# Emptying TensorE's banks on ScalarE, a norm folded into a sigmoid's scale, and two smaller edits in the mixers of a decoder layer

## The chip, the cores and the metric

The kernel runs on one core of a Trainium2 chip. The core has five engines that run side by side, each with its own queue that is worked off in order: TensorE (PE) for matrix products, VectorE (DVE), ScalarE (ACT), GpSimd (POOL), and SyncE (SP), which issues most of the DMAs. Matrix products land in eight banks of PSUM, 128 partitions by 512 fp32 numbers each; everything else lives in SBUF, and inputs, outputs and scratch rows in DRAM. The metric is the device time of one execution in microseconds (us); lower is better.

## The reference, cut to what matters

One decoder layer on 512 rows of width 1024, all in float32: a norm, one wide projection, two mixers side by side, a gated sum, an output projection, and an MLP.

```
h = rms_norm(x, norm_mix_g);  p = h @ w_in
q_a, k_a, v_a, o_a, i_a, f_a, q_b, k_b, v_b, g_a, g_b = split(p)
qk_a = silu(causal_conv([q_a, k_a], conv_w))            # 4 taps
h_a = mlstm_chunkwise(q_a, k_a, v_a, i_a, f_a)          # 8 heads
y_a = sigmoid(o_a) * head_rms_norm(h_a)
qn, kn = head_rms_norm(q_b), head_rms_norm(k_b)         # per row and head of 128
z = qn . kn / sqrt(128);  beta = sigmoid(z)             # s < t only
y_b[t] = sum_s beta_ts * prod_{s<j<t} (1 - beta_tj) * v_s
y = sigmoid(g_a) * y_a + sigmoid(g_b) * y_b
x = x + y @ w_out;  h2 = rms_norm(x);  x = x + relu(h2 @ w_up)**2 @ w_down
```

## The kernel before

All large products run in a split form: each fp32 operand is written as a rounded high part plus the rest, and a product is three matmuls (`mm3`, lines 111 to 114). A weight tile is therefore loaded (`raw`), cast to its high part on ACT (line 107, `whi`) and subtracted to its low part on DVE (line 108, `wlo`). `stage` does this for a quarter of a projection chunk (256 input rows by 512 columns). Its `raw` tiles rotate through the buffers in `load_pool`, at first two of the pool `wp`; the high and low parts have four buffers each. With `pool_raw` a call puts its `raw` tile elsewhere; the opening does that for the first two quarters of `va0`, with the pool `xp`.

`chunk` multiplies one chunk: four banks of the pool `ps_proj` (all that it has) gather the products over four quarters, so the next chunk can start only as banks are emptied.

The work runs in four parts. The opening norms and transposes x into `hT`, multiplies `va0` and forms the gates' decay rows; its pools `xp` and `cv` are closed at line 317, and the room is used again by later pools. The mixers then run in the order of the list `ORDER` (line 52): `qka` and `qkb` are the chunks of queries and keys of the first and second mixer, `r` decay rows, `m` a head of the first mixer, `n` the norm over four of its heads, `T` transposes for two heads of the second mixer, `s` a head of it, and `va`, `vb`, `oa`, `ga`, `gb` the remaining chunks. Then come the output projection and the MLP. The list sets in which order steps are emitted; a planner places the instructions in each engine's queue from its own model of their times, and work marked with `high_priority(offset=AHEAD)` may be placed far ahead of its place in the list. Where an engine waits, everything behind in its queue waits too.

The steps that the change touches:

- `qka` (327): ACT empties the four banks into `xc` (333); DVE applies the four taps (339, 341), ACT takes sigmoids (343), DVE multiplies (345), and both split the results into `qh`, `ql`, `kk` (354 to 359) for the heads `m`. `xc` takes the four buffers with the tag "nat".
- `qkb` (445): DVE empties the four banks into `nat` (451), the same four buffers; ACT squares (453), DVE sums per row and head (454), ACT takes the root (456), DVE the reciprocal (457), and DVE scales queries and keys, 512 columns at a time (460). The 512 columns are two heads' queries and two heads' keys.
- `sb_transpose`, `pair_T`: PE turns `nat` head by head; ACT and DVE scale by the learned gain and split (468, 469).
- `sb_head`: z for one head lies in three banks, as four segments of 512, 384, 128 and 256 columns (`SEG`), one for each block of 128 queries, which stand on the partitions. ACT takes sigmoid(-z) and sigmoid(z) bank by bank (484, 485); POOL masks, DVE scans (493) and multiplies (494), PE transposes and multiplies by v.
- `mlstm_norm` (414): four heads' norms as an 8 by 512 tile `dd`, with the root on ACT (435) and the reciprocal on DVE (436); the result goes to DRAM (438) and is read back spread over 128 partitions, one row per head (441), and multiplied in on DVE (442). These DMAs are issued from SP's queue, as the weights' are.

Of the kernel before, what the change touches and what calls it, by code (L numbers as in the profile page):

```python
# [8 lines left out]
F32 = mybir.dt.float32  # L9
F32R = mybir.dt.float32r  # L10
AF = mybir.ActivationFunctionType
ALU = mybir.AluOpType
# [4 lines left out]
P = 128  # L17
# [39 lines left out]
def block_kernel(ctx: ExitStack, tc: tile.TileContext, x, norm_mix_g, w_in, b_if, b_gate, conv_w, mlstm_norm_g,  # L57
# [37 lines left out]
    def stage(k2, srcs, name, ahead=None, pool_raw=None):  # L95

        with tc.high_priority(offset=AHEAD if ahead is None else ahead):
            p, tag, bufs = load_pool[len(staged) % len(load_pool)] if pool_raw is None else (pool_raw, "raw", 2)
            staged.append(name)
            raw = p.tile([P, 2, 512], F32, tag=tag, name=f"raw_{name}{k2}", bufs=bufs)  # L100
            for c, ap in srcs:
                n = ap.shape[-1]
                last["load"] = nc.sync.dma_start(out=raw[:, :, c:c + n],
                                                 in_=ap.rearrange("(kk p) n -> p kk n", p=P)).ins
            hi = wp.tile([P, 2, 512], F32R, tag="whi", name=f"whi_{name}{k2}")
            lo = wp.tile([P, 2, 512], F32R, tag="wlo", name=f"wlo_{name}{k2}")
            act.copy(hi, raw)  # L107
            dve.tensor_sub(lo, raw, hi.bitcast(F32))  # L108
        return hi, lo
# [6 lines left out]
    def chunk(name, src, transposed, lhs=None, staged=None, evac=None, gen=False):  # L116


        acc = []

        def one(o, k, wh, wl):
            kk, sl = k % 2, slice(o * P, (o + 1) * P)
            st, sp = k == 0, k == NK - 1
            if transposed:
                mm3(acc[o], wh[:, kk, sl], wl[:, kk, sl], hT[0][:, k, :], hT[1][:, k, :], st, sp)
            else:
                ah, al = (hT[0][:, k, sl], hT[1][:, k, sl]) if lhs is None else lhs(k, sl)
                mm3(acc[o], ah, al, wh[:, kk, :], wl[:, kk, :], st, sp)

        def new(o):  # L130
            acc.append(ps_proj.tile([P, S], F32, tag="pp", name=f"pp_{name}{o}"))

        if evac is not None:
            w = staged or [stage(k2, src(k2), name) for k2 in range(4)]
            def each():
                for o in range(4):
                    new(o)
                    for k in range(NK):
                        one(o, k, *w[k // 2])
                    evac(o, acc[o])  # L140
                    yield
            if gen:
                return each()
            list(each())
        else:
            for o in range(4):
                new(o)
            for k2 in range(4):
                w = stage(k2, src(k2), name)
                for k in (2 * k2, 2 * k2 + 1):  # L150
                    for o in range(4):
                        one(o, k, *w)
        return acc
# [48 lines left out]
    def col(i):  # L202
        return vec[:, i:i + 1]
# [46 lines left out]
    def gates(wg):  # L250
# [37 lines left out]
        act.activation(em, em, AF.Exp)  # L288
        return cc, rows, em

    v0, v1 = [], []

    def v_evac(got, name):
# [20 lines left out]
    pe.transpose(pv[:, :NV], vec_r, ident[:NV, :NV])  # L314
    dve.tensor_copy(vec, pv[:, :NV])
    dve.tensor_scalar_mul(vec[:, 56:57], vec[:, 56:57], float(P) ** -0.5)
    first.close()

    oh = cst.tile([P, 8, 8], F32, name="oh")
# [6 lines left out]

    def qka(i):

        accs = chunk(f"qka{i}", in_cols((C_QA + 256 * i, 256), (C_KA + 256 * i, 256)), True)
        with tc.high_priority(offset=AHEAD):  # L330
            xc = [t2("nat", 4, f"xc{i}{o}") for o in range(4)]
            for o, a in enumerate(accs):
                taken = act.copy(xc[o], a).ins
        y = [t2("sy", 8, f"cy{i}{o}") for o in range(4)]
        for j in range(4):
            for o in range(4):
                w = col(24 + (0, 4)[o // 2] + 2 * i + o % 2 + 8 * (3 - j))
                if j == 0:
                    dve.tensor_scalar_mul(y[o], xc[o], w)
                else:  # L340
                    dve.scalar_tensor_tensor(y[o][:, j:], xc[o][:, :S - j], w, y[o][:, j:], ALU.mult, ALU.add)
        for o in range(4):
            last_sig = act.activation(xc[o], y[o], AF.Sigmoid).ins
        for o in range(4):
            dve.tensor_mul(y[o], y[o], xc[o])


        qh, ql, kk = [], [], []
        for o in range(2):
            q = r4.tile([P, 2, S], F32R, tag="r4", name=f"qh{i}{o}")  # L350
            k = r4.tile([P, 2, S], F32R, tag="r4", name=f"kk{i}{o}")
            l = r4.tile([P, 2, S], F32R, tag="r4", name=f"ql{i}{o}")
            for w, (a, b) in enumerate(((L, H), (H, L))):
                act.copy(q[a, w, :], y[o][a, :])
                dve.tensor_copy(q[b, w, :], y[o][a, :])
                pool.memset(l[b, w, :].bitcast(F32), 0.0)
                dve.tensor_sub(l[a, w, :], y[o][a, :], q[a, w, :].bitcast(F32))
                act.copy(k[a, w, :], y[2 + o][a, :])
                dve.tensor_sub(k[b, w, :], y[2 + o][a, :], k[a, w, :].bitcast(F32))
            qh.append(q)  # L360
            ql.append(l)
            kk.append(k)
        return qh, ql, kk, last_sig, taken
# [50 lines left out]
    def mlstm_norm(h0, ssum):  # L414
        pd = bank(f"pd{h0}")
        for i in range(4):
            t = r5(f"dh{h0 + i}")[:, :D].rearrange("p (w n) -> p w n", w=2)
            split(t, ssum[i])
            for w in range(2):
                pe.matmul(pd[:8, :], oh_r[:, h0 + i, :], t[:, w, :], start=(i + w == 0), stop=(i + w == 4))  # L420
        dd = at.tile([8, S], F32, tag="dd", name=f"dd{h0}", bufs=1)
        act.activation(dd, pd[:8, :], AF.Abs)
        dve.tensor_max(dd, dd, em)
        dve.scalar_tensor_tensor(dd, dd, EPS, dd, ALU.mult, ALU.mult)
        pq = bank(f"pq{h0}")
        for i in range(4):
            sq = t2("jk", 1, f"sq{h0 + i}")
            act.activation(sq, ya[h0 + i], AF.Square)
            t = r5(f"sh{h0 + i}")[:, :D].rearrange("p (w n) -> p w n", w=2)
            split(t, sq)  # L430
            for w in range(2):
                pe.matmul(pq[:8, :], oh_r[:, h0 + i, :], t[:, w, :], start=(i + w == 0), stop=(i + w == 4))
        dve.scalar_tensor_tensor(dd, pq[:8, :], 1.0 / P, dd, ALU.mult, ALU.add)
        dve.tensor_scalar_max(dd, dd, float(2.0 ** -116))
        act.activation(dd, dd, AF.Sqrt)
        dve.reciprocal(dd, dd)
        rr = dram.tile([8, S], F32, name=f"rr{h0}")
        nc.sync.dma_start(out=rr, in_=dd)
        for i in range(4):
            rt = t2("g", 2, f"rt{h0 + i}")  # L440
            nc.sync.dma_start(out=rt, in_=rr[h0 + i:h0 + i + 1, :].partition_broadcast(P))
            dve.scalar_tensor_tensor(ya[h0 + i], ya[h0 + i], col(h0 + i), rt, ALU.mult, ALU.mult)


    def qkb(p):
        acc = chunk(f"qkb{p}", in_cols((C_QB + 256 * p, 256), (C_KB + 256 * p, 256)), False)
        nat, r = [], sm.tile([P, 4, 4], F32, tag="ssq", name=f"ssq{p}")
        for t in range(NT):
            n = t2("nat", 4, f"nat{p}{t}")
            with tc.high_priority(offset=AHEAD):  # L450
                dve.tensor_copy(n, acc[t])  # L451
            jk = t2("jk", 1, f"njk{p}{t}")
            act.activation(jk, n, AF.Square)
            dve.tensor_reduce(r[:, t, :], jk[:, :].rearrange("p (s d) -> p s d", s=4), AX.X, ALU.add)
            nat.append(n)
        act.activation(r, r, AF.Sqrt, scale=1.0 / P, bias=eps)
        dve.reciprocal(r, r)
        for t in range(NT):
            n3 = nat[t][:, :].rearrange("p (s d) -> p s d", s=4)
            dve.tensor_tensor(n3, n3, r[:, t, :].unsqueeze(2).to_broadcast([P, 4, P]), ALU.mult)  # L460
        return nat

    def sb_transpose(nat, s, g, name):
        pt = bank(f"pt_{name}")
# [5 lines left out]
        return q  # L470

    def pair_T(nat, p):
        return [[sb_transpose(nat, 2 * w + i, 56 + w, f"{'qk'[w]}T{2 * p + i}") for w in range(2)] for i in range(2)]

    def sb_head(h, q, k, v):

        z = half_square(f"zb{h}_")
        for j, o, n in SEG:
# [1 line left out]
            mm3(part(z, o, n), q[:, 0, il], q[:, 1, il], k[:, 0, :n], k[:, 1, :n], j != 3, True,  # L480
                skip_group_check=True)
        b, r = f5(f"b{h}"), f5(f"r{h}")
        for zz, c, n in z:
            act.activation(r[:, c:c + n], zz[:, :n], AF.Sigmoid, scale=-1.0)  # L484
            act.activation(b[:, c:c + n], zz[:, :n], AF.Sigmoid)  # L485
        for j, o, n in SEG:
            d = slice(o + n - P, o + n)
            pool.affine_select(out=b[:, d], in_=b[:, d], pattern=[[-1, P]], compare_op=ALU.is_gt, fill=0.0, base=0,  # L488
# [388 lines left out]
```

## Time and profile before

| | |
|---|---|
| time, median of 3 runs | 835.6 us (834.01 to 836.1) |
| the profiled execution: time | 834.67 us |
| the profiled execution: span, first to last instruction | 833.0 us |
| mean granted TensorE clock | 0.996 |
| DMA traffic | 113.64 MB, mean 136 GB/s |

The span in 40 equal slices of 20.8 us, in tenths of full use:

```profile
PE   8999799999999999999999999999999999999998
DVE  5577878767586686857843649798689868978994
ACT  6337475754549456545633437567356635655541
PEclk9999899999999999999999999999999999999999
DMA  8165533334430523431256415867988896898963
```

The mixers fill slices 2 to 23, the MLP the rest. A busy digit is an average over a slice: an engine can be nine tenths busy and still have one short gap, and whether a gap matters depends on whether PE stands still in it. The granted clock is the share of its full clock that TensorE was given in a stretch. In the views, a row of waits reads "who, on which line, waited for whom: us in total, times, longest".

### The profile page before, as it was taken

To read this page: it belongs to the slowest core of one execution; us is meant where nothing else is said; L and a number is where in the kernel's file an instruction comes from. 1 tells how busy PE (TensorE), PEld (TensorE's weight loads), DVE (VectorE), ACT (ScalarE), POOL (GpSimd) and SP (SyncE) were. 2 spreads that over 40 slices of the span, in tenths; PEclk is the share of its full clock that TensorE was granted. 3 is DMA by queue.
4 is the path that set the end of the run, shared out by engine and by line. 5 is a ranking of instruction groups with operands and counts; after the bars stand their busy time and mean duration, and the time that the engine had idled before them with its cause. 6 is when DMAs were issued, how large, how long until landed. Compare 5 with 4: busy or idle time off the path is not lost.

```text
span 833.0 us, 11490 instructions
## 1 busy us (share of the span) xinstructions
PE 812.9 (98%) x4366; PEld 696.4 (84%) x4366; DVE 611.0 (73%) x815; ACT 450.4 (54%) x656; POOL 157.4 (19%) x214
## 2 busy tenths in 40 slices
PE   8999799999999999999999999999999999999998
PEld 5878588788887787878888889898999999999876
DVE  5577878767586686857843649798689868978994
ACT  6337475754549456545633437567356635655541
POOL 3013223102220330001120101222402330332220
PEclk9999899999999999999999999999999999999999
DMA  8165533334430523431256415867988896898963
GB/s 209 49 155 175 109 78 70 75 104 76 141 119 15 147 85 76 126 98 56 77 202 240 118 22 149 180 142 181 205 228 175 168 196 199 174 193 183 233 127 103
DMA packets 63849, 113.64 MB, mean 136 GB/s; under 512 B 5225, under 2 KB 17561, under 8 KB 63794
## 3 DMA queue, kind: packets, MB, share of 16 engines
q1 hardware_dynamic: 44210, 71.42, 30.3%
q0 software_dynamic: 19584, 41.50, 26.2%
q8 instruction: 34, 0.56, 0.3%
q14 instruction: 21, 0.17, 0.1%
HBM read 110.73 MB, written 2.17 MB: 136 GB/s over the span
## 4 chain that ended last, share of the span: by engine, by line
PE 78%; DVE 9%; ACT 5%; DMA 5%; issue 3%; SPq 0%; POOL 0%; ACTq 0%; DVEq 0%
PE pp_yup L112 3%; PE pp_yup L113 3%; PE pp_yup L114 3%; PE pp_qkb L112 3%; PE pp_qkb L114 3%; PE pp_qkb L113 2%; PE ydn L113 2%; PE ydn L112 2%; PE ydn L114 2%; DMA raw_qkb<-in_w_in_dram 2%; PE pp_gb L112 2%; PE pp_zup L113 2%; PE pp_zup L112 2%; PE pp_ga L112 2%; PE pp_ga L113 2%
## 5 line engine op out<-in xcount | busy, mean ns | idle before, releaser
L112 PE MATMUL pp_qkb<-whi_qkb,hT 128*128 128x512 f32 x128 | 50.6, 401 | 3.8 <-DVE nat L451 3.8
L488 POOL TENSOR_SCALAR_AFFINE_SELECT b<-b 128x128 f32<-128x128 f32 x32 | 18.8, 609 | 171.9 <-ACT b L485 156.2
L113 PE MATMUL pp_qkb<-wlo_qkb,hT 128*128 128x512 f32 x128 | 50.7, 396 | 0.0
L114 PE MATMUL pp_qkb<-whi_qkb,hT 128*128 128x512 f32 x128 | 50.4, 397 | 0.0
L679 POOL DMA_DIRECT2D raw_Xup<-in_w_up_dram x24 | 29.2, 1247 | 91.4 <-DVE wlo_p5up L644 43.0
L679 POOL DMA_DIRECT2D raw_Xdn<-in_w_down_dram x18 | 21.9, 1234 | 102.5 <-DVE wlo_p1dn L644 53.1
L493 DVE TENSOR_TENSOR_SCAN r<-r,msk 128x512 f32<-128x512 f32 (+3 forms) x32 | 25.0, 835 | 13.0 <-ACT r L484 12.8
L112 PEld LDWEIGHTS pp_qkb<-whi_qkb,hT 128*128 128x128 f32 x128 | 24.6, 192 | 9.0 <-DVE nat L451 4.0
L108 DVE TENSOR_TENSOR wlo_qkb<-raw_qkb,whi_qkb 128x1024 fp32r<-128x1024 f32 x16 | 19.4, 1222 | 16.7 <-ACT whi_qkb L107 16.7
L113 PEld LDWEIGHTS pp_qkb<-wlo_qkb,hT 128*128 128x128 f32 x128 | 24.5, 192 | 5.3
L114 PEld LDWEIGHTS pp_qkb<-whi_qkb,hT 128*128 128x128 f32 x128 | 24.5, 191 | 5.3
L802 ACT ACTIVATE uq<-uq 128x512 f32<-128x512 f32 x32 | 19.8, 630 | 14.2 <-DVE uq L801 14.1
L107 ACT CAST whi_qkb<-raw_qkb 128x1024 fp32r<-128x1024 f32 x16 | 16.6, 1048 | 18.5 <-DMA raw_qkb<-in_w_in_dram 11.5
L112 PE MATMUL pp_va<-whi_va,hT 128*128 128x512 f32 x64 | 25.6, 404 | 0.5 <-ACT g_ga L528 0.5
L112 PE MATMUL pp_gb<-hT,whi_gb 128*128 128x512 f32 x64 | 24.9, 391 | 1.1 <-DVE vb L170 1.1
L114 PE MATMUL pp_va<-whi_va,hT 128*128 128x512 f32 x64 | 25.5, 399 | 0.0
L113 PE MATMUL pp_va<-wlo_va,hT 128*128 128x512 f32 x64 | 25.5, 399 | 0.0
L114 PE MATMUL pp_oa<-hT,wlo_oa 128*128 128x512 f32 x64 | 25.2, 393 | 0.0
L113 PE MATMUL pp_qka<-hT,whi_qka 128*128 128x512 f32 x64 | 25.2, 393 | 0.0
L113 PE MATMUL pp_ga<-hT,whi_ga 128*128 128x512 f32 x64 | 25.2, 393 | 0.0
L113 PE MATMUL pp_oa<-hT,whi_oa 128*128 128x512 f32 x64 | 25.1, 392 | 0.0
L112 PE MATMUL pp_qka<-hT,whi_qka 128*128 128x512 f32 x64 | 25.1, 395 | 0.0
(570 smaller groups left out, 2969.2 us busy)
## 6 DMA issues: line engine op xcount, KB each, us to landing
raw_Xup<-in_w_up_dram POOLq DMA_DIRECT2D x24, 512.0 KB, 7.7
raw_Xdn<-in_w_down_dram POOLq DMA_DIRECT2D x18, 512.0 KB, 6.7
raw_qkb<-in_w_in_dram SPq DMA_DIRECT2D x32, 256.0 KB, 4.1
rb<-rows POOLq DMA_DIRECT2D x8, 640.0 KB, 5.1
raw_va<-in_w_in_dram SPq DMA_DIRECT2D x8, 512.0 KB, 3.8
raw_qka<-in_w_in_dram SPq DMA_DIRECT2D x16, 256.0 KB, 4.6
raw_vb<-in_w_in_dram SPq DMA_DIRECT2D x8, 512.0 KB, 4.7
raw_oa<-in_w_in_dram SPq DMA_DIRECT2D x8, 512.0 KB, 4.7
```

What stands on the lines that cost most here:

```text
L107: act.copy(hi, raw)
L108: dve.tensor_sub(lo, raw, hi.bitcast(F32))
L112: pe.matmul(o, ah, bh, start=start, stop=False, **kw)
L113: pe.matmul(o, ah, bl, start=False, stop=False, **kw)
L114: pe.matmul(o, al, bh, start=False, stop=stop, **kw)
L488: pool.affine_select(out=b[:, d], in_=b[:, d], pattern=[[-1, P]], compare_op=ALU.is_gt, fill=0.0, base=0, channel_multiplier=1)
L493: dve.tensor_tensor_scan(kr, kr, msk[:, S - n:][:, ::-1], 1.0, ALU.mult, ALU.max)
L679: pool.dma_start(out=buf[b, j], in_=src(more, j), accum_op=ALU.add)
L802: act.activation(h(r, c), h(r, c), AF.Square)
```

## The change

Four edits, all between the opening and the output projection.

1. The weights of `qka0` are staged before the opening's pools are closed, with the second and fourth `raw` tile in `xp`'s buffers; `chunk` takes the staged tiles.
2. The banks of `qkb` are emptied by ACT instead of DVE. (In `qka`, ACT does so already; there the loops over taps are written differently, and issue the same instructions.)
3. The queries are no longer scaled by their norm before the transposes. The norm's reciprocal, and its negative, are kept in a small tile `rq` and given to the sigmoids as the scale of each partition, so that the sigmoids run segment by segment, eight a head. The keys are scaled as before, one head at a time.
4. In `mlstm_norm` the four rows in use go to DRAM and come back as 16 columns on 128 partitions; root and reciprocal are taken there, and the result goes to DRAM and is spread as before.

```diff
@@ chunk
-                w = stage(k2, src(k2), name)
+                w = staged[k2] if staged else stage(k2, src(k2), name)
@@ end of the opening
+    def qka_src(i):
+        return in_cols((C_QA + 256 * i, 256), (C_KA + 256 * i, 256))
...
+    qka0_w = [stage(k2, qka_src(0)(k2), "qka0", None, xp if k2 % 2 else None) for k2 in range(4)]
     first.close()
@@ qka
-        accs = chunk(f"qka{i}", in_cols((C_QA + 256 * i, 256), (C_KA + 256 * i, 256)), True)
+        accs = chunk(f"qka{i}", qka_src(i), True, staged=qka0_w if i == 0 else None)
...
@@ mlstm_norm
-        act.activation(dd, dd, AF.Sqrt)
-        dve.reciprocal(dd, dd)
-        rr = dram.tile([8, S], F32, name=f"rr{h0}")
-        nc.sync.dma_start(out=rr, in_=dd)
+        rd_, rr = (dram.tile([4, S], F32, name=f"{n}{h0}") for n in ("rd", "rr"))
+        dq = at.tile([P, 16], F32, tag="dq", name=f"dq{h0}")
+        nc.sync.dma_start(out=rd_, in_=dd[h0:h0 + 4, :])
+        nc.sync.dma_start(out=dq, in_=rd_.rearrange("h (a b) -> (h a) b", b=16))
+        act.activation(dq, dq, AF.Sqrt)
+        dve.reciprocal(dq, dq)
+        nc.sync.dma_start(out=rr.rearrange("h (a b) -> (h a) b", b=16), in_=dq)
         for i in range(4):
             rt = t2("g", 2, f"rt{h0 + i}")
-            nc.sync.dma_start(out=rt, in_=rr[h0 + i:h0 + i + 1, :].partition_broadcast(P))
+            nc.sync.dma_start(out=rt, in_=rr[i:i + 1, :].partition_broadcast(P))
@@ qkb
             with tc.high_priority(offset=AHEAD):
-                dve.tensor_copy(n, acc[t])
+                act.copy(n, acc[t])
...
+        rq = at.tile([P, 2, 4, 2], F32, tag="rq", name=f"rq{p}", bufs=3)
+        dve.tensor_copy(rq[:, 0], r[:, :, 0:2])
+        dve.tensor_scalar_mul(rq[:, 1], r[:, :, 0:2], -1.0)
         for t in range(NT):
-            n3 = nat[t][:, :].rearrange("p (s d) -> p s d", s=4)
-            dve.tensor_tensor(n3, n3, r[:, t, :].unsqueeze(2).to_broadcast([P, 4, P]), ALU.mult)
-        return nat
+            for s in (2, 3):
+                n = nat[t][:, s * P:(s + 1) * P]
+                dve.tensor_scalar_mul(n, n, r[:, t, s:s + 1])
+        return nat, rq
@@ sb_head
-        for zz, c, n in z:
-            act.activation(r[:, c:c + n], zz[:, :n], AF.Sigmoid, scale=-1.0)
-            act.activation(b[:, c:c + n], zz[:, :n], AF.Sigmoid)
+        for j, o, n in SEG:
+            for w, d in ((1, r), (0, b)):
+                act.activation(d[:, o:o + n], part(z, o, n), AF.Sigmoid, scale=rq[:, w, 3 - j, h % 2:h % 2 + 1])
```

More of the change, by code (lines that the diff above doesn't have):

```diff
@@ L334, in qka, with tap @@
         y = [t2("sy", 8, f"cy{i}{o}") for o in range(4)]
-        for j in range(4):
-            for o in range(4):
[L337 to L341, printed above, removed]
+        def tap(o, j):
+            return col(24 + (0, 4)[o // 2] + 2 * i + o % 2 + 8 * (3 - j))
+        for o in range(4):
+            dve.tensor_scalar_mul(y[o], xc[o], tap(o, 0))
+        for j in range(1, 4):
+            for o in range(4):
+                dve.scalar_tensor_tensor(y[o][:, j:], xc[o][:, :S - j], tap(o, j), y[o][:, j:], ALU.mult, ALU.add)
         for o in range(4):
@@ L472, in pair_T, with sb_head @@
     def pair_T(nat, p):
-        return [[sb_transpose(nat, 2 * w + i, 56 + w, f"{'qk'[w]}T{2 * p + i}") for w in range(2)] for i in range(2)]
-    def sb_head(h, q, k, v):
+        nat, rq = nat
+        return [[sb_transpose(nat, 2 * w + i, 56 + w, f"{'qk'[w]}T{2 * p + i}") for w in range(2)] + [rq]
+                for i in range(2)]
+    def sb_head(h, q, k, rq, v):
         z = half_square(f"zb{h}_")
```

## The prediction

> **What bounds the kernel now.** First the busy shares on the page, then the stretches by time, then what TensorE (PE) waited for in the stretch of the mixers, then the instructions around its longest wait.
>
> ```profile
> span 833.0 us, 11490 instructions
> PE 812.9 (98%) x4366; PEld 696.4 (84%) x4366; DVE 611.0 (73%) x815; ACT 450.4 (54%) x656; POOL 157.4 (19%) x214
> ```
>
> PE is busy for 98% of the span, and the change touches no matmul. So it can win only what PE loses: idle time, and time at a lowered clock.
>
> The stretches (columns: window, its length, busy time and instruction count of each engine, granted TensorE clock, DMA share, GB/s):
>
> ```profile
> 38.00:84.00 46.00, 46.00 (x203) 37.16 (x202) 34.90 (x54) 25.94 (x39) 10.54 (x23) 1.00 0.56 151
> 87.40:94.40 7.00, 1.88 (x11) 1.26 (x9) 6.75 (x11) 2.32 (x4) 0.00 (x0) 0.81 0.53 94
> 94.40:98.40 4.00, 4.00 (x10) 3.13 (x11) 3.97 (x6) 1.22 (x2) 1.09 (x2) 0.50 0.46 97
> 38.00:480.00 442.00, 433.97 (x2067) 359.53 (x2066) 310.03 (x413) 239.61 (x368) 75.37 (x124) 0.99 0.41 111
> 190.00:240.00 50.00, 50.00 (x254) 42.59 (x253) 32.05 (x41) 21.20 (x37) 13.51 (x27) 1.00 0.41 115
> ```
>
> In the mixers (38 to 480) PE is idle for 442.00 - 433.97 = 8.0 us. Of this 7.00 - 1.88 = 5.1 us lie between 87.4 and 94.4. The next 4.0 us ran at clock 0.50, which loses another 4.0 x 0.5 = 2.0 us. So one place costs 7.1 us, and all the rest of the mixers 2.9 us. The waits of PE in the mixers (total, times, longest) say the same:
>
> ```profile
> PE pp_qkb L112 <- DVE nat L451: 3.8, 1, 3.8
> PE za L390 <- DVE kk L359: 1.3, 1, 1.3
> PE pp_gb L112 <- DVE vb L170: 1.1, 1, 1.1
> PE pn L112 <- ACT ph L399: 1.1, 1, 1.1
> PE pp_va L112 <- ACT g_ga L528: 0.5, 2, 0.3
> PE zb L112 <- DVE qT L469: 0.3, 1, 0.3
> ```
>
> The first two are that place: qkb1 can't start until VectorE (DVE) has emptied qkb0's banks (L451), and the head before it waits for kk. The timeline there (start, us, engine, line, operation, tiles, then idle before and its releaser):
>
> ```profile
> 87.48 0.69 DVE L345 TENSOR_TENSOR cy<-cy,xc 128x512 f32<-128x512 f32 x1
> ...
> 89.49 1.05 ACT L107 CAST whi_qkb<-raw_qkb 128x1024 fp32r<-128x1024 f32 x1
> ...
> 93.65 2.47 DVE L451 COPY nat<-pp_qkb 128x512 f32<-128x512 f32 x4
> 94.36 0.63 ACT L453 ACTIVATE njk<-nat 128x512 f32<-128x512 f32 x1 [3.83 <-DVE nat L451]
> ```
>
> Between L345 and L451 DVE works without a break (6.75 of 7.00 us in the window above) on qka0's results and on weights, while ScalarE (ACT) sits idle for 3.83 us. The copy is late because it stands in a long DVE queue, not because it is long.
>
> **Bank copies on ACT (L451).** Rows of the groups by line and shape (busy us, mean ns):
>
> ```profile
> L333 ACT COPY xc<-pp_qka 128x512 f32<-128x512 f32 x8 | 4.7, 585 | 3.1 <-PE pp_qka L114 2.7
> L451 DVE COPY nat<-pp_qkb 128x512 f32<-128x512 f32 x16 | 10.5, 685 | 2.4 <-PE pp_qkb L114 1.7 <-PE pt_kT L466 0.7
> L460 DVE TENSOR_TENSOR nat<-nat,ssq 128x512 f32<-128x512 f32 x16 | 12.2, 815 | 0.1
> ```
>
> The same copy of a bank costs ACT 585 ns, DVE 685. Moved, it adds 16 x 0.585 = 9.4 us to ACT and takes 11.0 us off DVE. In qkb0 two things hold the copy back. The four nat buffers are those of xc, whose last reader is L345, ended at 88.2. And ACT may first do its casts, which end at 89.49 + 1.05 = 90.5. With the copy first, PE restarts at 88.2 + 0.6 = 88.8 at the latest; with the casts first, near 91.1. Against 94.4 that is 5.6 or 3.3 us. Either wait is shorter than the present one, and the waits of 1.1 us elsewhere come with clock 1.00 in their stretches, so I count the 2.0 us of lowered clock as gone. The place gives 5.3 to 7.1 us (all of it, where the copies stand ready behind other PE work).
> The Trainium skill, "ScalarE: Activation LUTs", Rules for kernel authors, says to leave plain adds, multiplies and maxima to VectorE rather than ScalarE; by the same sense the copies belong on DVE, and of this place only the earlier loads' part, some 4 us, would be left. The two rows disagree for this fp32 copy out of a bank, 585 against 685 ns, and they decide.
>
> **First weights in the opening's buffers (L149).** Two of qka0's four raw buffers come from the opening's pool, so that its loads needn't wait for each other. Eight DMAs issue as before, in the same SP queue, only behind the opening's loads instead of later. A row of ACT's waits, and three of its timeline, show what this frees:
>
> ```profile
> ACT whi_qka L107 <- DMA raw_qka<-in_w_in_dram: 4.0, 2, 2.4
> 69.99 1.05 ACT L107 CAST whi_qkb<-raw_qkb 128x1024 fp32r<-128x1024 f32 x1 [4.06 <-DMA raw_qkb<-in_w_in_dram]
> 70.95 0.58 ACT L333 COPY xc<-pp_qka 128x512 f32<-128x512 f32 x1
> 71.42 5.55 ACT L381 ACTIVATE rb<-rb,cc 128x512 f32<-128x512 f32 x12
> ```
>
> Two casts of qka0 waited 4.0 us together for loads; PE lost nothing by it (46.00 of 46.00 from 38 to 84). What counts is the 4.06 us behind them: the last qkb0 load was late, and the fourth xc copy stands behind its cast on ACT. With qka0's raw buffers free some 5 us sooner (those 4.0 and a cast), qkb0's loads start sooner too, and up to 4.1 us of that wait goes. Then convolution, sigmoid and kk end up to 4 us earlier, which removes the za wait of 1.3 us and lets L345 free the nat buffers before PE is done with qkb0. So this edit works on the same place as the first, and together they can take no more than its 7.1 us. From between I take 6.3, nearer the top, since both work on it. If the load stays late, the copy edit's 5.3 remains. The two buffers hold the opening's room until qka0 is cast; the decay rows that come to lie over it are first used at 71.4, so nothing waits for it. The rewritten loops of the convolution issue the same instructions in the same order, and cost nothing.
>
> **The norm of the queries.** Per chunk, four multiplies of 128x512 (L460) become eight of 128x128 on the keys, and two small ones for the scales. Prices of single-source multiplies:
>
> ```profile
> L339 DVE TENSOR_SCALAR cy<-xc,vec 128x512 f32<-128x512 f32 x8 | 3.7, 499 | 1.4 <-ACT xc L333 1.4
> 56.55 0.15 DVE L316 TENSOR_SCALAR vec<-vec 128x1 f32<-128x1 f32 x1
> ```
>
> Between them, a 128x128 one is 0.15 to 0.50 us; I take 0.15 + 0.35/4 = 0.24, proportional to width. 32 x 0.24 = 7.7, and 8 x 0.2 = 1.6 for the scales, against 12.2 us: DVE saves 2.9 (from +5.4 to -5.8 by the bounds). Query transposes no longer wait for the norm. The sigmoids (L484, L485) go from six to eight a head, each with a scale from memory:
>
> ```profile
> 159.58 0.60 ACT L484 ACTIVATE r<-zb 128x512 f32<-128x512 f32 x1
> ...
> 162.22 1.28 ACT L435 ACT_TABLE_LOAD   x1
> ```
>
> Six take 162.22 - 159.58 = 2.64 us now. The twelve exponentials of L381 above, in the same four widths and with an operand per partition, took 5.55 us, so four are 1.85 and eight 3.7. That is +1.06 a head, 8.5 us on ACT in all, and 1 us more before each head's transposes. What hides it is the projection matmuls that run between: from 190 to 240, with heads in it, PE lost nothing. Uncovered it would be up to 8.5 us.
>
> **The reciprocal over 128 partitions (n0, n4).** The rows, and the SP queue around both:
>
> ```profile
> L436 DVE RECIPROCAL dd<-dd 8x512 f32<-8x512 f32 x2 | 6.7, 3342 | 1.3 <-ACT dd L435 1.3
> L457 DVE RECIPROCAL ssq<-ssq 128x16 f32<-128x16 f32 x4 | 1.0, 247 | 0.4 <-ACT ssq L456 0.4
> 170.05 0.30 SPq L438 DMA_DIRECT2D rr<-dd  x1
> ...
> 172.12 1.06 SPq L441 DMA_DIRECT2D rt<-rr  x2
> ...
> 342.91 0.30 SPq L438 DMA_DIRECT2D rr<-dd  x1
> 344.37 0.83 SPq L441 DMA_DIRECT2D rt<-rr  x2
> wg_r<-in_w_in_dram SPq DMA_DIRECT2D x1, 64.0 KB, 13.0
> ```
>
> The DVE operation falls from 3.34 to 0.25 us, 6.2 in all. Two DMA hops are added (out, and back spread over 128 partitions). One hop, issue to the issue that waits for it, is 2.07 us at n0 and 1.46 at n4. So a chain gains 3.1 and loses 2.9 to 4.1: about even, up to +1.0. New waits: SP stands two hops longer before the next weight loads, ACT waits for a DMA at the root (casts of transposed weights behind it), DVE at the reciprocal (behind it the casts' remainders, and later qT, for which PE already waits 0.3 us). The far end for a hop in 64-byte pieces is wg_r's 13.0 us, which is eight times the bytes (64 KB against 8) behind the opening's megabytes in the same queue; the hop of dd itself, 16 KB between the same stages, is nearer, so I keep 1.5 to 2.1 and no loss.
> The Trainium skill, "DMA: Bandwidth & Descriptors", Specifications, has pieces under 512 B pay a read-modify-write; 64-byte pieces fall under it. No row of this kernel prices that at an idle queue; as a mechanism it is the rival of the longer round trip below.
>
> **Sum.** DVE in the mixers: -11.0 - 2.9 - 6.2 = -20 of 310 us; ACT +9.4 + 8.5 = +18 of 240. Both stay far under 442, so neither becomes the bound on average. PE: -6.3 at 87 to 98, the four other waits (3.0) unchanged in sum, and +0.5 for new small waits, since a planner lays out all queues anew: -5.8. Against the profiled execution, 833.0 span and 834.67 with what lies around it, this gives 828.9. That execution is 0.9 below the median of the runs, 835.6, so I forecast **829.8**, with 827 to 832 as its own range.
>
> **Rivals.**
> *All small waits go too* (DVE is 20 us lighter; the vb wait stands behind DVE's work): 7.1 + 3.0 = 10.1, so 825.5. Against it: they have four different causes, two of them on ACT. Chance 0.12.
> *Half of it*: the copies stand behind ACT's casts and kk, and the za wait stays; 3.3 us, or less with a new wait elsewhere: 832.3. For it: 88.2 as L345's end stays if the late load stays. Chance 0.18.
> *No gain, the change does not do what it says*: the planner puts copies behind exponentials or sigmoids (5.55 us in one go on ACT at 71.4), and PE waits as long, only for ACT: 835.6. Chance 0.13.
> *Slower*: the round trip of n0 and n4. If ACT stands at the root for both hops with the copies of transposed weights and qkb3's banks behind it, PE runs out: two waits of 4.1 us, each long enough for the lowered clock (2.0 more, as at 94.4), 12.2 - 5.8 = +6.4, so 842. It decides once a hop exceeds what PE has queued; at equal price the break-even is 2.9 us lost at each. By the page named above hops get longer and this is what would show. Against it: n0's chain today has 3.34 us in one piece and PE waits only 0.3 there. Chance 0.13.
> The forecast itself has 0.44.
>
> Differences under about 0.3%, 2.5 us, can't be told from no change here. Faster means below 833.1: 0.44 + 0.12 + two thirds of the half case, and a little of the rest: 0.69. Slower means above 838.1: 0.13 and a little of the third: 0.14. Same: 0.17. The range runs from 823.5 (every wait gone, with 2 us more for rows too coarse) to 837 (no gain), leaving out the slower case.
>
> **What would show it.** Right: clock 1.00 throughout 80 to 105, pp_qkb waiting under 1 us for ACT nat, the wait for raw_qkb before xc under 1 us, the reciprocal at 0.25 us and no PE wait over 1 us near n0 and n4. Wrong: a PE wait of 3 us or more anywhere in the mixers, a clock below 1 behind it, or zb waiting for sigmoids.

## Result and profile after

| | before | changed |
|---|---|---|
| time, median (range) | 834.89 us (834.01 to 836.1, 4 runs) | 825.49 us (824.51 to 825.58, 4 runs) |
| ratio to before, 95% interval | | 0.9892 [0.9878, 0.9906] |
| the profiled execution: time / span | 834.67 / 833.0 us | 825.4 / 823.3 us |

The changed kernel is 9.4 us faster. That lies inside the range, outside the forecast's own band of 827 to 832, and on the rival "all small waits go too" (825.5). The head of the page of the changed kernel, and its row of the granted clock in 40 slices:

```profile
span 823.3 us, 11511 instructions
...
PE 809.8 (98%) x4366; PEld 694.6 (84%) x4366; DVE 595.3 (72%) x823; ACT 458.0 (56%) x683; POOL 164.6 (20%) x214
...
PEclk9999999999999999999999999999999999999999
```

The one 8 in the clock row, the slice of qkb1, has gone. PE does the same 4366 matmuls. The stretches of the changed kernel (columns as in the prediction):

```profile
87.40:94.40 7.00, 7.00 (x35) 5.92 (x34) 6.91 (x10) 3.64 (x7) 2.94 (x4) 1.00 0.41 75
94.40:98.40 4.00, 4.00 (x25) 3.56 (x23) 3.30 (x5) 2.28 (x3) 1.38 (x2) 1.00 0.81 144
38.00:470.00 432.00, 430.57 (x2064) 357.71 (x2063) 294.34 (x421) 247.24 (x395) 82.61 (x124) 1.00 0.42 111
470.00:823.00 353.00, 345.33 (x2169) 311.03 (x2168) 282.19 (x370) 192.78 (x259) 75.27 (x62) 1.00 0.77 168
```

What was the hole at 87 to 98 is full (7.00 of 7.00, 4.00 of 4.00) at clock 1.00. Over the mixers, now 432 us long, PE is idle for 432.00 - 430.57 = 1.43 us, where it was 8.03. That is 6.6 us of idle time, and with the 2.0 us of lowered clock 8.6 of the 9.7 us by which the two spans differ. The output projection and the MLP, 353 us, kept their PE work within 0.3 us (345.09 of the same 353.00 before):

```profile
480.00:833.00 353.00, 345.09 (x2169) 311.16 (x2167) 282.26 (x370) 192.85 (x259) 75.27 (x62) 1.00 0.77 168
```

All that PE waited for in the mixers of the changed kernel, the whole answer of the view:

```profile
PE po L113 <- DVE al L521: 1.4, 1, 1.4
```

So the two waits at qkb1 are gone as forecast, but so are the four others (vb 1.1, ph 1.1, g_ga 0.5, qT 0.3), which the forecast had left standing. One wait is new. A second profile of the changed kernel (the run changed_again below) has this wait at 1.9 and two more of 0.3 and 0.2, so a difference of half a microsecond between the waits of two profiles says little. Two rows of ACT's timeline at qkb0's banks in the changed kernel show the copies (DVE's stood at 93.65):

```profile
85.32 0.59 ACT L461 COPY nat<-pp_qkb 128x512 f32<-128x512 f32 x1
86.48 1.54 ACT L461 COPY nat<-pp_qkb 128x512 f32<-128x512 f32 x3
```

The last copy ends at 86.48 + 1.54 = 88.0, 5.6 us before the old group began, and before PE starts qkb1 at 88.37.

### The profile page after: what moved, and what is told of

The parts are those of the page before. It is cut to its first block, busy times and chain, and to the rows that moved or that the text cites. A ratio compares the mean times of both kernels' runs of the same rounds, so it can differ in the third digit from the quotient of the medians.

```text
span 823.3 us, 11511 instructions
## 1 busy us (share of the span) xinstructions
PE 809.8 (98%) x4366; PEld 694.6 (84%) x4366; DVE 595.3 (72%) x823; ACT 458.0 (56%) x683; POOL 164.6 (20%) x214
## 4 chain that ended last, share of the span: by engine, by line
PE 91%; DVE 4%; DMA 3%; issue 1%; ACT 1%; SPq 0%; ACTq 0%; DVEq 0%
PE pp_qkb L114 4%; PE pp_qkb L112 4%; PE pp_qkb L113 4%; PE pp_yup L112 3%; PE pp_yup L113 3%; PE pp_yup L114 3%; PE ydn L112 2%; PE ydn L114 2%; PE ydn L113 2%; PE pp_qka L112 2%; PE pp_va L112 2%; PE pp_qka L113 2%; PE pp_va L113 2%; PE pp_va L114 2%; PE pp_zup L113 2%; PE pp_zup L112 2%
## 5 line engine op out<-in xcount | busy, mean ns | idle before, releaser
L114 PE MATMUL pp_qkb<-whi_qkb,hT 128*128 128x512 f32 x128 | 50.0, 393 | 0.0
L112 PE MATMUL pp_qkb<-whi_qkb,hT 128*128 128x512 f32 x128 | 49.3, 392 | 0.0
L108 DVE TENSOR_TENSOR wlo_qkb<-raw_qkb,whi_qkb 128x1024 fp32r<-128x1024 f32 x16 | 21.7, 1364 | 13.4 <-ACT whi_qkb L107 13.3
L112 PE MATMUL pp_ga<-hT,whi_ga 128*128 128x512 f32 x64 | 25.3, 395 | 0.0
L113 PE MATMUL pp_wo<-wlo_wo,y 128*128 128x512 f32 x64 | 25.1, 392 | 0.0
L113 PE MATMUL pp_ga<-hT,whi_ga 128*128 128x512 f32 x64 | 25.1, 392 | 0.0
```

The lines of the kernel that those rows point to most:

```text
L112: pe.matmul(o, ah, bh, start=start, stop=False, **kw)
L113: pe.matmul(o, ah, bl, start=False, stop=False, **kw)
L114: pe.matmul(o, al, bh, start=False, stop=stop, **kw)
```

## Experiments

Three questions. Are the gains of the four edits independent? Why did the vb, ph, g_ga and qT waits go? What is the new wait worth? The theory in front: edits 1 and 2 win the place at qkb1, and the small waits went because each of them hangs on a queue that two or more of the edits shorten. Its rivals: DVE is simply lighter, so that edit 3 or 4 alone would remove some of these waits; and the changed order of the planner's queues did it, with no single cause. The eight kernels with a single edit or without one keep the convolution's loops as they were, which issue the same instructions.

**Four single edits**, each put alone into the kernel before. Their cores:

```diff
only_staging:
+    qka0_w = [stage(k2, qka_src(0)(k2), "qka0", None, xp if k2 % 2 else None) for k2 in range(4)]
only_act_copies:
-                dve.tensor_copy(n, acc[t])
+                act.copy(n, acc[t])
only_sigmoid_scale:
+            act.activation(d[:, o:o + n], part(z, o, n), AF.Sigmoid, scale=rq[:, w, 3 - j, h % 2:h % 2 + 1])
only_reciprocal:
+        act.activation(dq, dq, AF.Sqrt)
+        dve.reciprocal(dq, dq)
```

> The kernel before with the first edit alone (qka0's weights staged in the opening's buffers). One-place theory (the gain is the single stop at qkb1's start, and edits 1 and 2 both work on it): the fourth xc copy comes about 4 us earlier, DVE ends its queue about 4 us earlier and still copies the banks, so PE restarts near 90.3 instead of 94.4 and the clock stays at 1.00: -4 to -6 us against before. Rival (the gain is DVE's lighter load, 20 us in the mixers): this edit takes no work off DVE, so at most -1 us.

> The kernel before with the second edit alone (qkb's banks emptied by ACT). One-place theory: PE restarts at 88.8 (copy ahead of ACT's casts) to 91.1 (behind them), the lowered clock goes: -5 to -7 us against before, and the late load of qkb0 stays visible as ACT's 4 us wait before the fourth xc copy. Rival (lighter DVE): 11 of the 20 us go, so about half of the 9.4 us, spread over several waits and not at one place.

> The kernel before with the third edit alone (queries' norm as the sigmoid's scale). One-place theory: nothing of the stop at qkb1's start goes, 0 +- 1 us against before. Rival (lighter DVE): -1 to -2 us. If the sigmoids' extra microsecond a head is not covered: up to +8 us.

> The kernel before with the fourth edit alone (root and reciprocal over 128 partitions). One-place theory: 0 +- 1 us against before; if the changed kernel's PE wait of 1.4 us for DVE al in n0 comes from the round trip, it shows here too and this edit alone is +1 to +2 us. Rival (lighter DVE): the vb wait of 1.1 us goes, -1 us.

**The changed kernel without one edit** (the same hunks taken back, one at a time):

```diff
without_staging:
-    qka0_w = [stage(k2, qka_src(0)(k2), "qka0", None, xp if k2 % 2 else None) for k2 in range(4)]
without_act_copies:
-                act.copy(n, acc[t])
+                dve.tensor_copy(n, acc[t])
without_sigmoid_scale:
+            dve.tensor_tensor(n3, n3, r[:, t, :].unsqueeze(2).to_broadcast([P, 4, P]), ALU.mult)
without_reciprocal:
+        act.activation(dd, dd, AF.Sqrt)
+        dve.reciprocal(dd, dd)
```

> The changed kernel without the first edit. One-place theory: as the copies alone, some -5 to -7 us against before (828 to 830), with ACT's 4 us wait for the last qkb0 load back. If the two edits only replace one another at that place, it is within 1 us of the changed kernel, 825 to 826.5.

> The changed kernel without the second edit: DVE empties qkb's banks. One-place theory: as the staging alone, -4 to -6 us against before (829 to 831). Lighter-DVE theory: 9 of the 20 us remain, about -4 us, but not at the stop of qkb1.

> The changed kernel without the third edit. One-place theory: within 1 us of the changed kernel, 824.5 to 826.5. If this edit is what removed the small waits near 255 and 274 us, those are back and it is 827 to 828.

> The changed kernel without the fourth edit. If the round trip causes the PE wait of 1.4 us for DVE al in n0, that wait goes and it is 823.5 to 824.5; if the edit is what removed the vb wait of 1.1 us near 355, that is back and the two cancel, 825 to 826.

Measured, with the waits of PE in the mixers (us, from the view of waits of one profiled execution of each kernel; the medians are over all its runs; "qkb1" is the wait of pp_qkb for nat, "za" for kk, "ph" that of pn for ph; waits of 0.2 are left out):

| kernel | median us | ratio [95%] | qkb1 | za | vb | ph | others |
|---|---|---|---|---|---|---|---|
| before (profile) | 834.9 | 1 | 3.8 | 1.3 | 1.1 | 1.1 | g_ga 0.5, qT 0.3 |
| only_staging | 829.85 | 0.9938 [0.9923, 0.9953] | 2.4 | - | 1.5 | 0.8 | g_ga 0.5, qT 0.4 |
| only_act_copies | 832.71 | 0.997 [0.9954, 0.9985] | - | 0.7 | 2.7 | 1.0 | g_ga 0.5 |
| only_sigmoid_scale | 841.5 | 1.0079 [1.0062, 1.0096] | 3.8 | 1.0 | 0.6 | 5.0 | qT 0.3 |
| only_reciprocal | 837.95 | 1.0036 [1.0023, 1.0049] | 3.8 | 0.6 | 2.8 | 1.0 | g_ga 0.5, qT 0.4 |
| without_staging | 828.0 | 0.9933 [0.9916, 0.995] | - | 1.3 | - | - | al 1.0, pl 0.5, nat 0.5 |
| without_act_copies | 829.21 | 0.9951 [0.9936, 0.9966] | 1.7 | - | 1.9 | - | qT 0.5 |
| without_sigmoid_scale | 825.27 | 0.9908 [0.9889, 0.9926] | - | - | 0.5 | 1.3 | g_ga 0.5, pl 0.5 |
| without_reciprocal | 829.25 | 0.996 [0.9945, 0.9975] | - | - | 2.5 | - | kT 2.1 |
| changed | 825.49 | 0.9892 [0.9878, 0.9906] | - | - | - | - | al 1.4 |

The medians of before beside them were 834.82 for the single edits and 833.23 for the four that leave one out. Against them, the single edits give -5.0, -2.1, +6.7 and +3.1: in sum +2.7, while together they give -9.4. Edits 3 and 4, each a loss alone, cost nothing or gain in company: by the ratios (each kernel to the before measured beside it) the changed kernel without edit 4 is slower by 0.68% (5.7 us), without edit 3 by 0.16%, within the intervals. Without edit 2 it loses 0.59% (4.9 us), without edit 1 0.41% (3.4).

*The place at qkb1.* DVE's timeline in only_staging:

```profile
89.62 2.47 DVE L455 COPY nat<-pp_qkb 128x512 f32<-128x512 f32 x4
```

The same group stood at 93.65: 4.03 us earlier, just the late load's 4.06. PE's wait shrank from 3.8 to 2.4 and the clock stayed up. PE's stretch there, then two of only_act_copies (window, length, PE busy, clock, DMA share, GB/s):

```profile
84.00:106.00 22.00, 19.64 (x95) 1.00 0.43 99
```

```profile
84.00:106.00 22.00, 21.07 (x99) 1.00 0.52 113
350.00:400.00 50.00, 47.33 (x235) 0.97 0.26 75
```

Alone, staging leaves 22.00 - 19.64 = 2.4 of the place's 7.1 us, and the whole kernel gains 5.0. The copies alone leave 22.00 - 21.07 = 0.9, so they win 6.2 there, but the kernel gains only 2.1. Its second row shows where the rest went: between 350 and 400 PE lost 2.67 us idle and 50 x 0.03 = 1.5 to the clock, where the kernel before lost 1.08 and none:

```profile
350.00:400.00 50.00, 48.92 (x248) 1.00 0.31 89
```

That is the wait for vb, grown from 1.1 to 2.7. So the first half of the theory holds, and the vb wait is where gains are given back.

*The vb wait.* It is 0.5 or none where edits 2 and 4 stand together (without_staging, without_sigmoid_scale, changed), and 0.6 to 2.8 elsewhere in the table; the 0.6, of edit 3 alone, can't be told from the 0.5. DVE at the end of n4 in only_reciprocal shows what holds vb:

```profile
355.36 0.75 DVE L446 SCALAR_TENSOR_TENSOR yq<-yq,vec,rt 128x512 f32<-128x512 f32 x1 [1.49 <-DMA rt<-rr]
356.03 1.88 DVE L170 TENSOR_TENSOR vb<-pp_vb,vb 128x512 fp32r<-128x512 f32 x3
```

vb's remainders stand in DVE's queue behind n4's multiplies, and these wait for a DMA of the norm. So n4's chain can set PE's wait. Since the kernels reach n4 at different times, the chain is measured from PE's last matmul of its squares (pq) to the issue of rr. In the changed kernel, PE, SP's queue and ACT:

```profile
324.15 0.40 PE L438 MATMUL pq<-sh,oh_r 128*8 128x512 f32 x1
```

```profile
325.75 0.27 SPq L444 DMA_DIRECT2D rd<-dd  x1
329.25 0.35 SPq L445 DMA_DIRECT2D dq<-rd  x1
332.79 0.33 SPq L448 DMA_DIRECT2D rr<-dq  x1
334.24 0.80 SPq L451 DMA_DIRECT2D rt<-rr  x2
```

```profile
330.97 1.28 ACT L446 ACT_TABLE_LOAD   x1
332.26 0.22 ACT L446 ACTIVATE dq<-dq 128x16 f32<-128x16 f32 x1
```

dd leaves 325.75 - 324.15 = 1.6 us behind the last square. The root has to wait for ACT in any case, which runs a head's sigmoids and squares and loads a table until 332.25; dq, 1.7 us on its way from 329.25, is there by then, and the root has no wait for a DMA in its row. Both hops lie beneath ACT's work, and rr goes out 332.79 - 324.15 = 8.6 us behind the last square. In only_reciprocal, PE and SP's queue:

```profile
330.59 0.39 PE L432 MATMUL pq<-sh,oh_r 128*8 128x512 f32 x1
```

```profile
337.12 0.27 SPq L438 DMA_DIRECT2D rd<-dd  x1
338.53 0.35 SPq L439 DMA_DIRECT2D dq<-rd  x1
341.58 0.33 SPq L442 DMA_DIRECT2D rr<-dq  x1
```

and DVE between the two:

```profile
331.87 1.28 DVE L455 COPY nat<-pp_qkb 128x512 f32<-128x512 f32 x2
...
334.38 0.67 DVE L433 SCALAR_TENSOR_TENSOR dd<-pq,dd 8x512 f32<-8x512 f32 x1
```

There dd leaves only 6.5 us behind the last square, because its steps stand behind copies of qkb's banks in DVE's queue; the hops lie open, and rr goes out after 11.0 us. With copies on ACT but the long reciprocal (without_reciprocal, last square at 324.91), dd is as early, but

```profile
333.16 3.34 DVE L440 RECIPROCAL dd<-dd 8x512 f32<-8x512 f32 x1 [1.47 <-ACT dd L439]
```

```profile
336.53 0.30 SPq L442 DMA_DIRECT2D rr<-dd  x1
```

(DVE's timeline, then SP's queue) rr goes out after 336.53 - 324.91 = 11.6 us. In the kernel before (PE), with rr issued at 342.91, it is 342.91 - 331.85 = 11.1:

```profile
331.85 0.39 PE L432 MATMUL pq<-sh,oh_r 128*8 128x512 f32 x1
```

The same difference in every profile of the table above:

| from the last pq to rr, n4 | us |
|---|---|
| before, only_staging, only_sigmoid_scale | 11.1, 11.1, 11.1 |
| only_act_copies, without_reciprocal (edit 2, not 4) | 11.6, 11.6 |
| only_reciprocal, without_act_copies (edit 4, not 2) | 11.0, 11.0 |
| without_staging, without_sigmoid_scale, changed (both) | 8.6, 8.6, 8.6 |

Neither edit shortens the chain alone; both together take 2.5 us off it. The rival "DVE is lighter" falls with the two tables: edits 3 and 4 each take work off DVE, and each alone makes the kernel slower. What is not explained by the chain is how large the wait is among the kernels with 11 us (0.6 to 2.8); only_reciprocal's has rt DMAs that took 3.5 to 6.6 us to land, 3.0 to 4.6 before, and in only_act_copies DVE has 2.6 us of the norm's multiplies of nat and 1.2 us of a weight's low part among and behind the four multiplies, ahead of vb.

This holds for n4 alone. At n0 the two hops lie open in the changed kernel, as ACT's row of the root shows:

```profile
159.58 0.22 ACT L446 ACTIVATE dq<-dq 128x16 f32<-128x16 f32 x1 [3.10 <-DMA dq<-rd]
```

There the chain from the last square to the first loads of rt is as long with edit 4 as without it: 163.75 - 152.22 = 11.5 us in the changed kernel, 164.45 - 152.87 = 11.6 in without_reciprocal.

**Edits 2 and 4 alone together** test this reading: alone they give -2.1 and +3.1, but with the hops covered they should gain more than edit 2 does.

```diff
-                dve.tensor_copy(n, acc[t])
+                act.copy(n, acc[t])
...
+        act.activation(dq, dq, AF.Sqrt)
+        dve.reciprocal(dq, dq)
```

> The kernel before with edits 2 and 4 together. Alone they gave -2.1 and +3.1 us, so if edits add up this is +1. Theory of the covered round trip (with the banks emptied by ACT, DVE has n4's row sums ready early, and the two new hops run while ACT is at its sigmoids; without that they lie open): PE's wait for vb before gb0, 2.7 and 2.8 us in the two single runs, is at most 0.7 us here, the wait at qkb1's start stays as in the copies alone (1 to 2 us), the waits of 250 to 275 us stay (2 us): -4 to -6 us against before.

Measured: 829.07 us, ratio 0.9927 [0.9914, 0.9941] to 835.07 of before: -6.0 where the single edits add up to +1.0. Its waits:

```profile
PE pn L112 <- ACT ph L399: 1.1, 1, 1.1
PE pn L113 <- DVE pl L400: 0.6, 2, 0.4
PE pp_gb L112 <- DVE vb L170: 0.5, 1, 0.5
PE pp_va L112 <- ACT g_ga L532: 0.5, 2, 0.3
PE za L390 <- DVE kk L359: 0.5, 1, 0.5
PE zb L112 <- DVE qT L473: 0.4, 1, 0.4
```

The vb wait is 0.5, where it was 2.7 and 2.8 with either edit alone, and rr goes out 335.90 - 327.27 = 8.6 us behind the last square here too. The reading held, with 0.5 us of the wait left. The waits for ph and g_ga are untouched: they belong to another cause. The table shows which edit they go with: every kernel of it without edit 3 has ph at 0.8 to 1.3 and g_ga at 0.5, and the kernels with edit 3 in company have neither. When edit 3 was left out they came back, as was expected if this edit had removed them; the time, 825.27 us, stayed all the same, and the wait for al was gone instead.

**Hold the multiplies back.** If vb waits only because n4's multiplies stand ahead of it, then moving these and their rt loads behind vb1's last split must remove the wait, in the kernel before as well. In n0 they are held until the last split of T1, past the al of the new wait. Done to the changed kernel and to the kernel before, with the changed kernel run again beside them:

```diff
-            dve.scalar_tensor_tensor(ya[h0 + i], ya[h0 + i], col(h0 + i), rt, ALU.mult, ALU.mult)
+        def spread():
...
+                dve.scalar_tensor_tensor(ya[h0 + i], ya[h0 + i], col(h0 + i), rt, ALU.mult, ALU.mult)
+        return spread
...
+                with tc.issue_after(last["v"]):
+                    got["n4"]()
```

> The changed kernel with the four multiplies by the spread norm (and their loads) held until T1's last split for n0 and vb1's last split for n4, so that DVE's queue has them behind al and vb instead of ahead. If that place in the queue is the cause of the changed kernel's last wait in the mixers (po for DVE al, 1.4 us), the wait goes: -1.5 us against the changed kernel, span 821 to 822. Rival: the gates of oa0 then wait for the norm and PE for their banks, and the time is the changed kernel's or worse.

> The kernel before with the same hold and nothing else. If the multiplies ahead of vb and qT in DVE's queue cause the waits for vb (1.1 us) and qT (0.3 us), both go and the stop at qkb1's start stays: -1.5 us against before. If the vb wait is ACT's (its casts end at 355), it stays and the time is that of before.

> The changed kernel on this chip, to set beside the one with the later multiply: ratio to before 0.988 to 0.991, and 1.5 us above the later multiply if the theory holds.

Measured against 835.07 us: later_multiply 825.4, ratio 0.9897 [0.9881, 0.9912]; later_multiply_before 833.57, 0.9985 [0.9974, 0.9996]; changed_again 824.95, 0.9879 [0.9861, 0.9897]. All waits of PE in the mixers of later_multiply, and those of later_multiply_before:

```profile
PE pp_qka L112 <- ACT g_oa L546: 2.5, 1, 2.5
```

```profile
PE pp_qkb L112 <- DVE nat L453: 3.8, 1, 3.8
PE pp_qka L112 <- ACT g_oa L529: 2.4, 1, 2.4
PE za L390 <- DVE kk L359: 0.2, 1, 0.2
```

In the kernel before, the waits for vb and qT vanish as the mechanism asks. But more than half of what goes (4.1 us of waits in all) is given back in a new wait of 2.4 us, and the kernel is 1.5 us faster by the medians: the gates of oa0 take the same buffers as rt, and ACT waits 3.4 us ahead of two of them for the multiplies now held back. In the changed kernel the new wait for al (1.4) goes and the one for g_oa (2.5) comes: no time is gained, and no version here beats the changed kernel. In later_multiply_before the waits at ph and g_ga are also gone, without edit 3. So that part of the rival stands: those two waits follow from the order of the queues, which an edit elsewhere can lay out anew. Edit 3 alone removed the wait for g_ga and made the one for ph worse. Its PE stretch there:

```profile
250.00:280.00 30.00, 24.78 (x103) 0.89 0.29 83
```

It lost 5.2 us idle and some 30 x 0.11 = 3.3 to the clock (the idle part of the stretch counts in that mean, so this is an upper figure), where the kernel before lost 1.5 and none, with PE waiting 5.0 us for ph while ACT went on with casts and va copies. Why the planner chose that order was not settled.

## Why the prediction came out as it did

The sign, the place and its mechanism were right; one term was mis-sized, the sum of the small waits.

- *What bounds the kernel.* Right. 8.6 of the 9.7 us between the spans are PE's idle time and lowered clock in the mixers.
- *Copies on ACT, 5.3 to 7.1 us at the place.* Right: alone 6.2 there. What the step did not see is that 3.1 of it are given back at 350 to 400 if n4's chain stays as it is. It also counted the lowered clock as gone for any shorter wait; that held because no wait was left there, but with a wait of 1.7 us (without_act_copies) the clock fell to 0.50. By the rule named in the prediction (plain operations to VectorE; the Trainium skill, "ScalarE: Activation LUTs", Rules for kernel authors) the copies would have stayed on DVE, which is without_act_copies: 829.21 us, 0.59% slower than the changed kernel. For these copies the runs speak against carrying the rule over, and by more than the price of the copies themselves (685 - 589 = 96 ns each, 1.5 us in all, against 4.9): the rest shows as waits behind DVE's queue, 1.7 us for the banks and 1.9 for vb.
- *First weights staged earlier, "up to 4.1 us of that wait goes".* Right: 4.03 us. Both together took the whole 7.1, not 6.3.
- *The norm of the queries.* Its price was near. Rows of the groups by line and shape in the changed kernel:

```profile
L475 DVE TENSOR_SCALAR nat<-nat,ssq 128x128 f32<-128x128 f32 x32 | 8.8, 346 | 0.0
L461 ACT COPY nat<-pp_qkb 128x512 f32<-128x512 f32 x16 | 8.4, 589 | 4.5 <-PE pp_qkb L114 4.5
```

  The 128x128 multiply took 0.35 us in the mean, not 0.24. All of DVE's busy time fell by 611.0 - 595.3 = 15.7, not 20; ACT's rose by 458.0 - 450.4 = 7.6, not 18. The sigmoids did come to 34.7 us by their rows, 8.8 more than before (forecast 8.5), but ACT loaded five tables fewer (5 x 1.28 = 6.4 us): two for its exponentials where it had been five, and none for the sigmoids of ga, which in the kernel before stand among exponentials and cost two. The rest of the difference was not traced. That the projection matmuls hide it holds in company, where the edit's 0.16% can't be told from nothing. Alone it cost 6.7 us, but no sigmoid was waited for: the loss was the new order at 250 to 275.
- *The reciprocal, "about even, up to +1.0".* Here the working failed, at n4. For the chain with the copies on DVE it is exact: 11.0 us to rr against 11.1; and at n0 too, 11.5 against 11.6. But the chain of n4 was priced as it stood before. With the copies on ACT the hops lie under ACT's work there and the shorter reciprocal is left as a gain: 8.6 against 11.6. Leaving the edit out costs 5.7 us by the ratios, 3.7 between the two profiles, where PE waits 2.5 us for vb and 2.1 for kT instead of 1.4 for al.
- *"The four other waits (3.0) unchanged in sum, and +0.5 for new small waits".* This is the step that failed: 3.0 went and 1.4 came. The vb wait fell to 0.5 through edits 2 and 4 together (shown; the last 0.5 is within what two profiles of one kernel differ by); ph and g_ga went with edit 3 in company, through the new order of the queues (shown to move with it, the cause of the order not). The rival that all of them go was forecast with "DVE is 20 us lighter" as its reason; its time was right, its reason was not.
- *"No PE wait over 1 us near n0 and n4".* Right at n4, wrong at n0: the new 1.4 us. The changed kernel on DVE there:

```profile
166.96 0.75 DVE L452 SCALAR_TENSOR_TENSOR yq<-yq,vec,rt 128x512 f32<-128x512 f32 x1 [4.97 <-DMA rt<-rr]
167.63 0.68 DVE L521 TENSOR_TENSOR al<-zt,ah 128x512 fp32r<-128x512 f32 x1
```

  The al that PE needs stands behind a multiply which waits for rt. This is not the "slower" rival, though the place is its own: PE waits for DVE at the multiply, not for ACT at the root, and rt is loaded as late without the round trip. In without_reciprocal the first multiply waits 4.79 us for rt, but al stands ahead of it; there the last multiply, at 177.38, waits 2.64 us for its rt and holds kT behind it, and PE waits 2.1 us for kT. Which of the two waits PE meets is a matter of the order of DVE's queue.

Five of my own expectations missed as well. The copies alone were to give 5 to 7 us and gave 2.1, since the wait for vb grew. Edit 3 alone was to change nothing and cost 6.7, without a wait for its sigmoids; edit 4 alone was to cost at most 2 us, through the wait for al, and cost 3.1, with the wait for vb grown instead. without_reciprocal was to keep nearly all of the gain and lost 5.7 us of it, and holding the multiplies back won nothing in the changed kernel. The fourth showed what edit 4 is worth beside edit 2; the fifth that the wait could be moved, not removed.

## What to carry to other kernels

Price a longer round trip by what its consumer waits for anyway: at n4 two hops beneath a wait that was there already cost nothing, and the same two hops in the open cost as much as the shorter reciprocal saved. Where queues run in order, try small edits in company, by leaving one out, before you drop one that loses alone: here four edits add up to +2.7 us singly and to -9.4 together. And when a wait is removed by moving work behind it, look who shares that work's buffers.

## What the runs showed of the hardware

The hop of 8 KB in 64-byte pieces (rr from dq) takes longer at n0 than at n4. SP's queue in the changed kernel at n0, from the issue of rr to that of the rt that waits for it:

```profile
160.11 0.33 SPq L448 DMA_DIRECT2D rr<-dq  x1
163.75 0.79 SPq L451 DMA_DIRECT2D rt<-rr  x2
```

163.75 - 160.11 = 3.64 us, against 334.24 - 332.79 = 1.45 at n4 (rows above). The profiles with edit 4 have it at 2.3 to 3.4 us from issue to landing at n0, and at n4 at 1.4, once at 2.3. So small pieces alone do not set the time. Nor does the core's other traffic: its DMA engines were 5% busy from 160.1 to 163.3 and 7% from 332.8 to 334.2. What differs between the two places was not tried. The prediction had kept 1.5 to 2.1 a hop; the 2.2 us more at n0 lengthen the chain on which the new wait for al hangs. The hop before it, dd's 8 KB to DRAM, is the other way round: 157.85 - 156.44 = 1.41 us at n0, and 329.25 - 325.75 = 3.50 at n4, where the DMA engines were 78% busy.

The granted clock fell after waits shorter than the 3.8 us of before, but not after every one. A PE stretch behind the 1.7 us wait of without_act_copies:

```profile
92.00:94.00 2.00, 2.00 (x6) 0.50 0.14 43
```

and one behind the 2.4 us wait of only_staging:

```profile
92.00:94.00 2.00, 2.00 (x11) 1.00 0.10 37
```

The shorter wait lowered the clock to half, the longer one did not. The Trainium skill, "TensorE: Matmul & The Clock Gate", HAM oscillation, warns of idle gaps above some 3.4 us; these runs show half clock behind one gap of half that length. There the 1.7 us of waiting cost another 2.00 x 0.5 = 1.0 us in this row alone, so a short wait can cost more than itself, and its length alone does not tell.
